# Operand addresses, matmul order and raw buffers in a hybrid decoder layer's kernel

## The chip, the cores and the metric

The kernel runs on one core of a Trainium2 chip. The metric is the device time of one execution in microseconds (us). A core has the engines TensorE (PE; its weight loads are shown apart as PEld), VectorE (DVE), ScalarE (ACT) and GpSimd (POOL), each with its own queue of instructions, and SyncE (SP), whose queue here issues the loads from memory. The engines wait for one another on semaphores.

## The reference

One decoder layer on 256 tokens of width 2048, all in float32, cut to what matters here:

```python
h = rmsnorm(x, g_mix) @ w_in                 # 2048 x 5728
z, xbc, dt, q, k, v, qi, ki, wi = _split(h, IN_SIZES)
y_ssd = gated_norm(ssd(silu(conv(xbc)), dt), z)      # 16 heads of 64
ki = rmsnorm(ki, g_kidx)                     # key of the indexer, 64 wide
y_att = dsa_attention(rmsnorm(q), rmsnorm(k), v, qi, ki, wi)   # top 64 keys
x = x + concat([y_ssd, y_att]) @ w_out       # 2048 x 2048
u = rmsnorm(x, g_mlp) @ w_up                 # 2048 x 8192
return x + square(relu(u)) @ w_down          # 8192 x 2048
```

## The kernel before

**Precision.** A float32 product is made of three products of the fast type fp32r: each operand is split into a high half (rounded) and a low half (the rest), and high·high + high·low + low·high is summed in PSUM.

**Weights.** All 400 weight tiles of the kernel come through `operands` (L110), mostly 128 x 1024 (512 KB). It has SP issue the load of `raw` (L119), ScalarE cast the high half `whi` (L122), and VectorE subtract the low half `wlo` (L123). `raw` has RB = 4 buffers, `whi` and `wlo` have WB = 5 each. So the load of a tile waits until VectorE has made the low half of the tile four before it, and the casts wait for matmuls that free `whi`. These steps have a higher priority than the rest in a scheduler that orders SP's, ScalarE's and VectorE's instructions by times of its own; TensorE's order is the order of the code.

**Products.** `product` (L126) takes the weights as the moving operand, 512 (or 304) columns, with activations loaded as 128 x 128 stationary blocks (L141 to L143). `product_t` (L168) does the reverse: a unit of 256 output columns has four tiles of eight 128 x 128 weight blocks, loaded as the stationary operand, and the activations stream past. The activations are kept as [high | low], 256 tokens each: a high weight block times both halves is one matmul of 512 columns (L181), a low block times the high half one of 256 columns (L182). A "pair" below is these two; a unit has 32 pairs.

**Stages on TensorE.** Input product in blocks: k and m0 (straight `product`; m0 is 304 wide and holds `ki`, `wi`, `dt` and part of `v`), qi (4 units) and xbc (6 units) by `product_t`, then m1, q0, q1, z0, z1 straight. Between them run the norms, the indexer, the state space part and attention, as tasks whose TensorE work enters at counted steps (`step`, the table `Y`). Then the output product (w_out), and the two layers of the MLP in quarters: `up(0)`, `up(1)`, `down(0)`, `up(2)`, `down(1)`, `up(3)`, `down(2)`, `down(3)`. `up` is 8 units of `product_t` per quarter (the very first is made ahead), `down` is straight with 512 columns.

**Addresses.** In a partition, all `whi` and `wlo` buffers start at the same byte modulo 256, as do the activations of w_out and of the down product (`yah`, `ysh`, `uh`, `ul`). `hx` (the activations of the input product) and `x2x` (those of the up product, in the same place) start 64 bytes past it.

**From m0 to qi.** After m0, ScalarE evacuates `sm0` and `sm1` (L306, scaled by `rstd`, the norm of x, which VectorE ends with L282), squares the indexer's keys (`kj`, L365, sum `kss`), VectorE turns that into a reciprocal root (`rx_ki`, L273 to L282, some dozen small operations) and writes the normed keys `kd` (L371). After the first unit of qi TensorE transposes them (`ps_ki`, L376).

Of the kernel before, what the change touches and what calls it, by code (L numbers as in the profile page):

```python
# [9 lines left out]
F32 = mybir.dt.float32  # L10
F32R = mybir.dt.float32r
# [5 lines left out]
P = 128  # L17
D = 2048
T = 256
NB = T // P  # L20
KT = D // P
# [6 lines left out]
HP = 600  # L28
WARM = 9
WB = 5  # L30
RB = 4


Z0, XBC0, DT0, Q0, K0, V0, QI0, KI0, WI0, END = (
# [31 lines left out]
def hymba_kernel(ctx: ExitStack, tc: tile.TileContext, xn, xt, w_in, w_out, w_up, w_down, vcol, vrow, out):  # L66
    nc = tc.nc
    ctx.enter_context(tc.manual_schedule(engines={nc.tensor.engine}))
    keep = ctx.enter_context(tc.tile_pool(name="keep", bufs=1))
    wts = ctx.enter_context(tc.tile_pool(name="wts", bufs=1))  # L70
# [24 lines left out]
    def step():  # L95
        for t in list(tasks):
            if isinstance(t[1], int) and t[1] > 0:
                t[1] -= 1
            elif not isinstance(t[1], str) or t[1] in done:
                advance(t)  # L100
# [6 lines left out]
        return vc[:, VC[name] + i:VC[name] + i + 1]  # L107


    def operands(src, n, load=None):  # L110

        with tc.high_priority(offset=HP):
            raw = wts.tile([P, n], F32, name="raw", tag="raw", bufs=RB)
            hi = wts.tile([P, n], F32R, name="whi", tag="whi", bufs=WB)
            lo = wts.tile([P, n], F32R, name="wlo", tag="wlo", bufs=WB)
            step = n if load is None else n // 2
            for i in range(0, n, step):
                s = slice(i, i + step)
                nc.sync.dma_start(raw[:, s], src[:, s])  # L119
                if load is not None:  # L120
                    load()
                nc.scalar.copy(hi[:, s], raw[:, s])  # L122
                nc.vector.tensor_tensor(lo[:, s], raw[:, s], hi[:, s].bitcast(F32), op=OP.subtract)  # L123
        return hi, lo
# [4 lines left out]
    def accumulators():  # L129
        return [ps.tile([P, 512], F32, name="acc", tag="acc") for _ in range(2)]  # L130

    def product(src, n, left, load=None, tail=None):
# [16 lines left out]
        for kt in range(KT):  # L149
            if kt % 2 == 0:  # L150
                hi, lo = operands(src[kt // 2], 2 * n, load)
            w = slice(kt % 2 * n, kt % 2 * n + n)
            wh, wl = hi[:, w], lo[:, w]
            if kt < last:
                part(kt, acc[0][:, :n], 0, wh, wl)
                if tail is None:
                    part(kt, acc[1][:, :n], 1, wh, wl)
                else:
                    for i, (b, c) in enumerate(halves):
                        part(kt, acc[1 + i][:, c], b, wh[:, c], wl[:, c])  # L160
            else:
                kept.append((kt, wh, wl))
            step()
# [4 lines left out]
                tail(b, c, acc[i][:, c])  # L168
        return acc

    def product_t(src, right):

        acc = accumulators()
        for i in range(4):
            hi, lo = operands(src[i], 1024)
            c = i % 2
            for k in range(8):
                kt = 8 * (i // 2) + k
                x = right(kt)
                s = slice(k * P, (k + 1) * P)  # L180
                nc.tensor.matmul(acc[c], hi[:, s], x, start=(kt == 0), stop=False)  # L181
                nc.tensor.matmul(acc[c][:, T:], lo[:, s], x[:, :T], start=False, stop=(kt == KT - 1))  # L182
                if k % 4 == 3:
                    step()
        return acc

    def total(dst, acc):

        for c in range(2):
            nc.scalar.copy(dst[:, c, :], acc[c][:, T:])  # L190
            nc.vector.tensor_tensor(dst[:, c, :], acc[c][:, :T], dst[:, c, :], op=OP.add)
# [9 lines left out]


    vc = keep.tile([P, NVC], F32, name="vc")
    hx = keep.tile([P, KT, 2 * T], F32R, name="hx")
    room = keep.tile([P, 4096], F32, name="room", tag="xr")
    
    x_done = []
# [29 lines left out]
    for name, cols in IN_BLOCKS:  # L237
        n = sum(b - a for a, b in cols)
# [8 lines left out]
    def in_pair(name, i):  # L247
        o = in_off[name][0] + i * 256 * D
        return product_t(w_in[o:o + 256 * D].rearrange("(h p c) -> h p c", h=4, p=P), lambda kt: hx[:, kt, :])
# [501 lines left out]
    def x2(kt):  # L751
        if kt >= KT - 4:
            need("res3")
        return box[0][:, kt, :]

    first = product_t(w_up[0], x2)
    while tasks:
        step()
# [11 lines left out]
    def up(q):  # L770
        uh = mlp.tile([P, KT, T], F32R, name="uh")
        ul = mlp.tile([P, KT, T], F32R, name="ul")
        for j in range(8):
            r = mlp.tile([P, 2, T], F32, name="r")
            total(r, first if q + j == 0 else product_t(w_up[8 * q + j], x2))
            nc.vector.scalar_tensor_tensor(r, r, 0.0, r, op0=OP.max, op1=OP.mult)
            s = slice(2 * j, 2 * j + 2)
            nc.scalar.copy(uh[:, s, :], r)
            nc.vector.tensor_tensor(ul[:, s, :], r, uh[:, s, :].bitcast(F32), op=OP.subtract)
        return uh, ul  # L780

    def down(q, u):
        for j in range(4):
# [9 lines left out]
            for b in range(0 if end else NB):  # L793
                add(b, slice(0, 512), acc[b])

    u = [up(0)]
    for q in range(1, 4):
        u.append(up(q))
        down(q - 1, u[q - 1])
# [53 lines left out]
```

## Time and profile before

| | |
|---|---|
| median of 3 runs | 1112.9 us (1112.73 to 1113.47) |
| the profiled execution | 1111.47 us, its span 1109.4 us |
| TensorE busy | 1100.4 us (99%) |
| VectorE, ScalarE, GpSimd busy | 692.4, 535.0, 41.4 us |
| weight loads, 512 KB, issue to landing (median) | 3.6 to 4.0 us |
| memory read | 204.29 MB, 186 GB/s over the span |

A row's duration for a matmul includes its way through the array, so neighbours overlap: a 512-column matmul is printed with 0.39 us while the next one starts 0.23 us later. Pace is therefore taken from start to start. In a timeline, equal instructions in a row may be one row with a count (x4) and the time that they take together; idle time before a row and what ended it stand in brackets.

### The profile page before, as it was taken

How to read it: one execution, taken by the hardware profiler on the slowest of the kernel's cores; microseconds unless marked ns; L12 is line 12 of the kernel's file. 1: busy time of each engine (PE TensorE's matmuls, PEld its weight loads, DVE VectorE, ACT ScalarE, POOL GpSimd, SP SyncE). 2: the span in 40 equal slices, each digit the busy share in tenths (PEclk: the TensorE clock that was granted, in tenths of full speed). 3: DMA queues.
4: the chain of work that ended last, by engine and by line, in shares of the span. 5: the costliest groups of instructions: out<-in, count | busy, mean ns of one | idle time of the engine just before them, and what ended most of it. 6: DMA issues, size and time to landing. Idle time of an engine off the chain costs nothing.

```text
span 1109.4 us, 14959 instructions
## 1 busy us (share of the span) xinstructions
PE 1100.4 (99%) x5686; PEld 937.9 (85%) x5686; DVE 692.4 (62%) x976; ACT 535.0 (48%) x749; POOL 41.4 (4%) x41
## 2 busy tenths in 40 slices
PE   9999998999999999999999999999999999999998
PEld 7988887888888888888888888888888888888887
DVE  6886989667765565656565456565555565554443
ACT  7755645556765454444443334444434444333431
POOL 0010131112000000000000000000000000000000
PEclk9999999999999999999999999999999999999999
DMA  9855435644375555556656655655666556665662
GB/s 327 270 195 175 152 106 175 194 147 134 115 256 185 184 181 184 187 189 189 183 186 198 193 190 190 191 190 190 192 192 191 188 188 191 198 195 191 209 212 73
DMA packets 63735, 207.36 MB, mean 187 GB/s; under 512 B 7216, under 2 KB 11568, under 8 KB 63664
## 3 DMA queue, kind: packets, MB, share of 16 engines
q1 hardware_dynamic: 63520, 206.36, 58.1%
q8 instruction: 45, 0.74, 0.3%
q14 instruction: 26, 0.21, 0.1%
q10 hardware_dynamic: 144, 0.05, 0.0%
HBM read 204.29 MB, written 2.10 MB: 186 GB/s over the span
## 4 chain that ended last, share of the span: by engine, by line
PE 92%; DVE 4%; DMA 1%; issue 1%; ACT 1%; SPq 0%; POOL 0%; ACTq 0%; DVEq 0%
PE acc L181 27%; PE acc L141 16%; PE acc L142 16%; PE acc L143 16%; PE acc L182 14%; DVE wlo L123 1%; DVE bc L495 1%; PE ps_y L566 1%; DVE sc L459 1%; DMA xrow<-in_xn 1%; PE ps_sr L650 0%; PE ps_l L604 0%; PE ps_o L629 0%; ACT xrow L230 0%; DMA raw<-in_w_in 0%
## 5 line engine op out<-in xcount | busy, mean ns | idle before, releaser
L123 DVE TENSOR_TENSOR wlo<-raw,whi 128x1024 fp32r<-128x1024 f32 (+3 forms) x400 | 466.9, 1170 | 380.9 <-ACT whi L122 377.7
L122 ACT CAST whi<-raw 128x1024 fp32r<-128x1024 f32 (+3 forms) x400 | 400.5, 1004 | 497.4 <-PE acc L142 248.7
L181 PE MATMUL acc<-x2x,whi 128*128 128x512 f32 x1024 | 359.9, 395 | 0.0
L182 PE MATMUL acc<-x2x,wlo 128*128 128x256 f32 x1024 | 287.8, 281 | 0.0
L181 PEld LDWEIGHTS acc<-x2x,whi 128*128 128x128 f32 x1024 | 192.5, 188 | 45.4
L142 PE MATMUL acc<-whi,ul 128*128 128x512 f32 (+1 forms) x512 | 197.6, 386 | 0.0
L141 PE MATMUL acc<-whi,uh 128*128 128x512 f32 (+1 forms) x512 | 197.5, 386 | 0.0
L143 PE MATMUL acc<-wlo,uh 128*128 128x512 f32 (+1 forms) x512 | 197.5, 386 | 0.0
L182 PEld LDWEIGHTS acc<-x2x,wlo 128*128 128x128 f32 x1024 | 192.0, 188 | 0.1
L181 PE MATMUL acc<-hx,whi 128*128 128x512 f32 x320 | 114.0, 397 | 0.0
L141 PEld LDWEIGHTS acc<-whi,uh 128*128 128x128 f32 x512 | 96.1, 188 | 19.5
L143 PEld LDWEIGHTS acc<-wlo,uh 128*128 128x128 f32 x512 | 96.1, 188 | 19.5
L142 PEld LDWEIGHTS acc<-whi,ul 128*128 128x128 f32 x512 | 96.2, 188 | 19.2
L182 PE MATMUL acc<-hx,wlo 128*128 128x256 f32 x320 | 90.0, 281 | 0.0
L143 PE MATMUL acc<-wlo,hx 128*128 128x512 f32 (+1 forms) x224 | 83.0, 370 | 3.1 <-DVE wlo L123 3.1
L141 PE MATMUL acc<-whi,hx 128*128 128x512 f32 (+1 forms) x224 | 85.4, 381 | 0.1
L142 PE MATMUL acc<-whi,hx 128*128 128x512 f32 (+1 forms) x224 | 82.6, 369 | 0.0
L181 PEld LDWEIGHTS acc<-hx,whi 128*128 128x128 f32 x320 | 60.3, 188 | 13.5
L182 PEld LDWEIGHTS acc<-hx,wlo 128*128 128x128 f32 x320 | 60.1, 188 | 0.0
L143 PEld LDWEIGHTS acc<-wlo,hx 128*128 128x128 f32 x224 | 42.0, 187 | 12.0 <-DVE wlo L123 4.7
L141 PEld LDWEIGHTS acc<-whi,hx 128*128 128x128 f32 x224 | 42.2, 188 | 7.7 <-issue 0.7
L142 PEld LDWEIGHTS acc<-whi,hx 128*128 128x128 f32 x224 | 42.1, 188 | 7.4 <-issue 0.7
(224 smaller groups left out, 828.4 us busy)
## 6 DMA issues: line engine op xcount, KB each, us to landing
raw<-in_w_up SPq DMA_DIRECT2D x128, 512.0 KB, 3.7
raw<-in_w_down SPq DMA_DIRECT2D x128, 512.0 KB, 4.0
raw<-in_w_in SPq DMA_DIRECT2D x72, 512.0 KB, 3.6
raw<-in_w_out SPq DMA_DIRECT2D x32, 512.0 KB, 3.6
raw<-in_w_in SPq DMA_DIRECT2D x16, 256.0 KB, 4.2
raw<-in_w_in SPq DMA_DIRECT2D x16, 152.0 KB, 5.3
raw<-in_w_in SPq DMA_DIRECT2D x8, 304.0 KB, 2.9
xT<-in_xt SPq DMA_DIRECT2D x16, 128.0 KB, 4.1
```

The source lines that it names most:

```text
L122: nc.scalar.copy(hi[:, s], raw[:, s])
L123: nc.vector.tensor_tensor(lo[:, s], raw[:, s], hi[:, s].bitcast(F32), op=OP.subtract)
L141: nc.tensor.matmul(out, ah[:, s], wh, start=(kt == 0), stop=False)
L142: nc.tensor.matmul(out, al[:, s], wh, start=False, stop=False)
L143: nc.tensor.matmul(out, ah[:, s], wl, start=False, stop=(kt == KT - 1))
L181: nc.tensor.matmul(acc[c], hi[:, s], x, start=(kt == 0), stop=False)
L182: nc.tensor.matmul(acc[c][:, T:], lo[:, s], x[:, :T], start=False, stop=(kt == KT - 1))
L459: nc.vector.scalar_tensor_tensor(sc[:, :nk], rl[:, i, :nk], wis[:, b, h:h + 1], neg[:, T - nk:] if first else sc[:, :nk], op0=OP.mult, op1 ...
L495: nc.vector.scalar_tensor_tensor(o[:, j, :], pad[:, j, k:k + T], vcp("conv_w", 12 * k + ct), o[:, j, :], op0=OP.mult, op1=OP.add)
L566: nc.tensor.matmul(pt[:, 64 * i:64 * i + 64], m[i // 4][:, i % 4, :], xdt[:, c, 64 * h:64 * h + 64], start=True, stop=True)
```

## The change

Three things change together.

1. **Address.** Two spare tiles in the pool, `gap0` (192 bytes) and `gap1` (64 bytes), put `hx`, and `x2x` after it, at the same byte modulo 256 as the weights. Every `whi` and `wlo` buffer gets 64 floats more; its data can start 0, 64, 128 or 192 bytes into it.
2. **The up product.** `product_t` takes a `shift` (unit j: 64·(j mod 4) bytes) and an `order`, one for each four units. H is a high block with 512 columns, l a low block with 256; X and L are the two 256-column halves of H, each with its own load of the weights. "Hl" is the order of before, "HHHHHHHHllllllll" makes the eight high matmuls of a tile and then the eight low ones. The input product keeps "Hl" and shift 0.
3. **Buffers.** `raw` has 3 buffers instead of 4, which pays for the spare floats.

```diff
--- before.py
+++ after.py
@@ -28,7 +28,11 @@
 HP = 600
 WARM = 9
 WB = 5
-RB = 4
+RB = 3
+SPARE = 64
+
+
+ORDERS = ["Hl", "HHHHHHHHllllllll", "HllH", "HHHHllll", "XLl", "XlL", "LXl", "HHll"]
 
 
 Z0, XBC0, DT0, Q0, K0, V0, QI0, KI0, WI0, END = (
@@ -107,12 +111,12 @@
         return vc[:, VC[name] + i:VC[name] + i + 1]
 
 
-    def operands(src, n, load=None):
+    def operands(src, n, load=None, shift=0):
 
         with tc.high_priority(offset=HP):
             raw = wts.tile([P, n], F32, name="raw", tag="raw", bufs=RB)
-            hi = wts.tile([P, n], F32R, name="whi", tag="whi", bufs=WB)
-            lo = wts.tile([P, n], F32R, name="wlo", tag="wlo", bufs=WB)
+            hi = wts.tile([P, n + SPARE], F32R, name="whi", tag="whi", bufs=WB)[:, shift:shift + n]
+            lo = wts.tile([P, n + SPARE], F32R, name="wlo", tag="wlo", bufs=WB)[:, shift:shift + n]
             step = n if load is None else n // 2
             for i in range(0, n, step):
                 s = slice(i, i + step)
@@ -168,19 +172,26 @@
                 tail(b, c, acc[i][:, c])
         return acc
 
-    def product_t(src, right):
+    def product_t(src, right, shift=0, order=ORDERS[0]):
 
         acc = accumulators()
         for i in range(4):
-            hi, lo = operands(src[i], 1024)
+            hi, lo = operands(src[i], 1024, None, shift)
             c = i % 2
-            for k in range(8):
-                kt = 8 * (i // 2) + k
-                x = right(kt)
-                s = slice(k * P, (k + 1) * P)
-                nc.tensor.matmul(acc[c], hi[:, s], x, start=(kt == 0), stop=False)
-                nc.tensor.matmul(acc[c][:, T:], lo[:, s], x[:, :T], start=False, stop=(kt == KT - 1))
-                if k % 4 == 3:
+            w = {"H": hi, "X": hi, "L": hi, "l": lo}
+            out = {"H": slice(0, 2 * T), "X": slice(0, T), "L": slice(T, 2 * T), "l": slice(T, 2 * T)}
+            part = {"H": slice(0, 2 * T), "X": slice(0, T), "L": slice(T, 2 * T), "l": slice(0, T)}
+            n = order.count("l")
+            for g in range(0, 8, n):
+                seen = dict.fromkeys("HXLl", 0)
+                for at, o in enumerate(order):
+                    k = g + seen[o]
+                    seen[o] += 1
+                    kt = 8 * (i // 2) + k
+                    nc.tensor.matmul(acc[c][:, out[o]], w[o][:, k * P:(k + 1) * P], right(kt)[:, part[o]],
+                                     start=(i < 2 and g == 0 and at == 0),
+                                     stop=(i >= 2 and g + n == 8 and at == len(order) - 1), skip_group_check=True)
+                for _ in range((g + n) // 4 - g // 4):
                     step()
         return acc
 
@@ -201,7 +212,9 @@
 
 
     vc = keep.tile([P, NVC], F32, name="vc")
+    keep.tile([P, 48], F32, name="gap0")
     hx = keep.tile([P, KT, 2 * T], F32R, name="hx")
+    keep.tile([P, 16], F32, name="gap1")
     room = keep.tile([P, 4096], F32, name="room", tag="xr")
     
     x_done = []
@@ -772,7 +785,7 @@
         ul = mlp.tile([P, KT, T], F32R, name="ul")
         for j in range(8):
             r = mlp.tile([P, 2, T], F32, name="r")
-            total(r, first if q + j == 0 else product_t(w_up[8 * q + j], x2))
+            total(r, first if q + j == 0 else product_t(w_up[8 * q + j], x2, 16 * (j % 4), ORDERS[2 * q + j // 4]))
             nc.vector.scalar_tensor_tensor(r, r, 0.0, r, op0=OP.max, op1=OP.mult)
             s = slice(2 * j, 2 * j + 2)
             nc.scalar.copy(uh[:, s, :], r)
```

**How it moves instructions: the entry to qi.** The scheduler orders VectorE and ScalarE anew. On VectorE, from the last step of `rstd` on (`wlo` are low halves, the first 1024-wide one is qi's first tile; `rx_ki` starts the norm of the keys), before:

```order
L282 TENSOR_TENSOR rstd<-rt_x,ry_x 128x2
L123 TENSOR_TENSOR wlo<-raw,whi 128x1024
L298 TENSOR_SCALAR dg<-ident,rstd 128x128 x2
L340 TENSOR_TENSOR s_361<-s_361,rstd 128x8
L123 TENSOR_TENSOR wlo<-raw,whi 128x1024
L340 TENSOR_TENSOR s_361<-s_361,rstd 128x8
L123 TENSOR_TENSOR wlo<-raw,whi 128x1024 x2
L372 TENSOR_SCALAR wis<-sm_106,rstd 128x16
L412 TENSOR_TENSOR dt<-sm_106,vr 128x16
L123 TENSOR_TENSOR wlo<-raw,whi 128x1024
L273 TENSOR_SCALAR rx_ki<-kss 128x2
```

and after, from the instruction behind `rstd` on:

```order
L311 TENSOR_SCALAR dg<-ident,rstd 128x128 x2
L353 TENSOR_TENSOR s_363<-s_363,rstd 128x8 x2
L127 TENSOR_TENSOR wlo<-raw,whi 128x1024 x4
L385 TENSOR_SCALAR wis<-sm_108,rstd 128x16
L385 TENSOR_SCALAR wis<-sm_109,rstd 128x16
L425 TENSOR_TENSOR dt<-sm_108,vr 128x16
L425 TENSOR_TENSOR dt<-sm_109,vr 128x16
L427 SCALAR_TENSOR_TENSOR sp_a<-dt 128x32
L127 TENSOR_TENSOR wlo<-raw,whi 128x1024
L440 TENSOR_SCALAR dt<-dt 128x32
L127 TENSOR_TENSOR wlo<-raw,whi 128x1024
L286 TENSOR_SCALAR rx_ki<-kss 128x2
```

The first low half of qi stood directly behind `rstd`; now `dg` and both scalings of `s` stand ahead of it. Up to `rx_ki` there were five low halves, now there are six.

ScalarE at the same place, from the evacuation of `sm0` on (`whi` are the high halves, here those of qi's fifth tile and later; `kj` are the squares of the keys), before:

```order
L306 ACTIVATE sm0_106<-acc_373,rstd_103 128x96
L306 ACTIVATE room_88<-acc_373,rstd_103 128x208
L122 CAST whi_778<-raw_777 128x1024
L306 ACTIVATE sm1_107<-acc_374,rstd_103 128x96
L306 ACTIVATE room_88<-acc_374,rstd_103 128x208
L365 ACTIVATE kj_586,kss_108<-sm0_106 128x64
L365 ACTIVATE kj_588,kss_108<-sm1_107 128x64
L122 CAST whi_800<-raw_799 128x1024
```

and after:

```order
L319 ACTIVATE sm0_108<-acc_375,rstd_105 128x96
L319 ACTIVATE room_90<-acc_375,rstd_105 128x208
L319 ACTIVATE sm1_109<-acc_376,rstd_105 128x96
L126 CAST whi_780<-raw_779 128x1024
L319 ACTIVATE room_90<-acc_376,rstd_105 128x208
L378 ACTIVATE kj_588,kss_110<-sm0_108 128x64
L126 CAST whi_802<-raw_801 128x1024
L378 ACTIVATE kj_590,kss_110<-sm1_109 128x64
```

The cast of `whi_802` (`whi_800` before, the sixth tile of qi) stood behind both `kj` and now stands between them. The loads on SP keep their order, but each waits for the low half of three tiles before it.

**And: the start of `up(2)` on TensorE**, the last matmuls of `down(0)` and the first of the unit (numbers are buffers), before:

```order
L141 MATMUL acc_5921<-whi_6049,uh_3994 128x512
L142 MATMUL acc_5921<-whi_6049,ul_3995 128x512
L143 MATMUL acc_5921<-wlo_6050,uh_3994 128x512
L181 MATMUL acc_6071<-x2x_3383,whi_6074 128x512
L182 MATMUL acc_6071<-x2x_3383,wlo_6075 128x256
```

and after:

```order
L145 MATMUL acc_5923<-whi_6051,uh_3996 128x512
L146 MATMUL acc_5923<-whi_6051,ul_3997 128x512
L147 MATMUL acc_5923<-wlo_6052,uh_3996 128x512
L191 MATMUL acc_6073<-x2x_3385,whi_6076 128x256 x2
L191 MATMUL acc_6073<-x2x_3385,wlo_6077 128x256
```

The matmul of 512 columns has become two of 256, in the twelve units with X and L: 384 matmuls and weight loads more.

## Rows read from the trace of the kernel before

**Rows 1.** The page: engines' busy us (share) x instructions, and clock of 40 slices in tenths.

```profile
PE 1100.4 (99%) x5686; PEld 937.9 (85%) x5686; DVE 692.4 (62%) x976; ACT 535.0 (48%) x749; POOL 41.4 (4%) x41
...
PEclk9999999999999999999999999999999999999999
```

**Rows 2.** Waits of TensorE: line, waited for, us in total, times, longest.

```profile
PE acc L143 <- DVE wlo L123: 3.1, 3, 1.8
...
PE ps_ki L376 <- DVE kd L371: 0.5, 1, 0.5
```

**Rows 3.** Timeline, TensorE, z1's last matmuls: start us, us, engine, line, op, out<-in, shape.

```profile
301.21 0.39 PE L141 MATMUL acc<-whi,hx 128*128 128x512 f32 x1
...
304.01 0.39 PE L141 MATMUL acc<-whi,hx 128*128 128x512 f32 x1
```

**Rows 4.** Timeline, TensorE, inside `down(0)`.

```profile
591.13 0.39 PE L141 MATMUL acc<-whi,uh 128*128 128x512 f32 x1
...
595.21 0.39 PE L141 MATMUL acc<-whi,uh 128*128 128x512 f32 x1
```

**Rows 5.** Timeline, TensorE, start of the output product.

```profile
305.80 0.40 PE L142 MATMUL acc<-whi,yal 128*128 128x512 f32 x1
...
307.89 0.39 PE L142 MATMUL acc<-whi,yal 128*128 128x512 f32 x1
...
312.42 0.39 PE L141 MATMUL acc<-whi,yah 128*128 128x512 f32 x1
```

**Rows 6.** Timeline, TensorE, pairs of qi.

```profile
46.77 0.40 PE L181 MATMUL acc<-hx,whi 128*128 128x512 f32 x1
...
52.43 0.39 PE L181 MATMUL acc<-hx,whi 128*128 128x512 f32 x1
```

**Rows 7.** High-half matmuls of up(0)-up(1), then up(3), by line: count, durations, first-last start.

```profile
L181 PE MATMUL acc<-x2x,whi x372: 392/397/398, 446.7 to 577.8; 128*128 128x512 f32 x186
...
L181 PE MATMUL acc<-x2x,whi x256: 392/392/398, 841.6 to 930.6; 128*128 128x512 f32 x128
```

**Rows 8.** Timeline, TensorE, 256-column matmuls at the kernel's end.

```profile
1102.91 0.28 PE L141 MATMUL acc<-whi,uh 128*128 128x256 f32 x1
...
1105.66 0.28 PE L143 MATMUL acc_t<-wlo,uh 128*128 128x256 f32 x1
```

**Rows 9.** Timeline, SP's queue, the weight loads from m0 into qi.

```profile
31.85 0.80 SPq L119 DMA_DIRECT2D raw<-in_w_in  x2
...
35.08 21.84 SPq L119 DMA_DIRECT2D raw<-in_w_in  x12
```

**Rows 10.** Timeline, ScalarE, high halves of the weights and the key norm.

```profile
38.46 1.05 ACT L122 CAST whi<-raw 128x1024 fp32r<-128x1024 f32 x1 [0.93 <-DVE ry_x L282]
40.53 1.05 ACT L122 CAST whi<-raw 128x1024 fp32r<-128x1024 f32 x1 [1.02 <-DMA raw<-in_w_in]
...
43.23 1.06 ACT L122 CAST whi<-raw 128x1024 fp32r<-128x1024 f32 x1 [0.23 <-DMA raw<-in_w_in]
...
47.21 0.25 ACT L365 ACTIVATE kj<-sm 128x64 f32<-128x64 f32 x1
```

**Rows 11.** Timeline, VectorE, low halves, key norm and `kd`.

```profile
34.19 1.63 DVE L123 TENSOR_TENSOR wlo<-raw,whi 128x304 fp32r<-128x304 f32 x4
...
37.48 0.85 DVE L123 TENSOR_TENSOR wlo<-raw,whi 128x304 fp32r<-128x304 f32 x2
...
39.93 1.23 DVE L123 TENSOR_TENSOR wlo<-raw,whi 128x1024 fp32r<-128x1024 f32 x1
...
47.69 0.16 DVE L273 TENSOR_SCALAR rx_ki<-kss 128x2 f32<-128x2 f32 x1
...
53.42 0.41 DVE L371 TENSOR_SCALAR kd<-sm,krs 128x64 f32<-128x64 f32 x2
```

**Rows 12.** Timeline, TensorE, the first matmuls of the kernel.

```profile
1.26 4.16 PE L200 MATMUL ps_w<-ones 128*128 128x128 f32 x18 [1.26 <-POOL ones L195]
...
5.54 0.50 PE L142 MATMUL acc<-whi,hx 128*128 128x512 f32 x1
```

## The prediction

> **What bounds the kernel now.** I read the page first: TensorE is busy 99% of the span, and the granted clock stands at its top digit in every slice [rows 1]. So an edit counts only if it changes how long TensorE's own matmuls take, or if it makes TensorE wait. Next come the waits of TensorE: three of 3.1 us in all on VectorE's low halves of the weights, and one of 0.5 us at the transposes of `kd` [rows 2]. Everything else TensorE has in time. The rest is read as pace: the distance from the start of one matmul to the start of the next, since the printed duration overlaps the neighbour.
>
> Three paces matter. With `hx` as the moving operand, 64 bytes past the weights' place in 256, twelve matmuls of 512 columns take 304.01 − 301.21 = 2.80 us, 233.3 ns each [rows 3]. In the down product, where activations and weights have the same place, eighteen take 4.08 us, 226.7 ns [rows 4]. The difference, 6.6 ns, is what the new addresses are worth at most. It isn't had at once: after the transposes ahead of the output product, where the places are also equal, the first nine take 2.09 us (232 ns), the next twenty 4.53 us (226.5) [rows 5].
>
> **The offsets in the input products.** `hx` moves to the weights' place. The straight blocks after the m1 block have 384 matmuls of 512 columns (q0, q1, z0, z1). All at the lower pace is 384 × 6.6 ns = 2.5 us. But work of other kinds (transposes, attention) interrupts them some 24 times in TensorE's order, and each time about nine run at 232: 216 × 1.3 ns + 168 × 6.6 ns = 1.4 us. I take −1.4, with 0 and −2.5 as ends. The 96 of the k block gain 0.6 us, which is worth nothing: what follows waits for VectorE (below). The 320 pairs of qi and xbc take 353.8 ns at first (16 in 5.66 us) [rows 6]. Locked, a pair would be 226.7 + 120 = 346.7. I take half of that gap, 3.3 ns, for the 288 pairs behind the wait below: −0.95, ends 0 and −2.0.
>
> **The pairs of the up product.** Of its 32 units of 32 pairs, 16 (quarters 0 and 1) now run at 131.1/371 = 353.4 ns a pair, 16 (quarters 2 and 3) at 89.0/255 = 349.0 [rows 7], all with one offset and one order. Since one offset has two paces, offset alone doesn't set it. Afterwards 20 units stay unsplit, in four orders and four offsets. The ends for the 16 early ones are the locked pair, 512 × 6.7 ns = −3.4 us, and a pace as much worse, +3.4; I take half the gain, −1.7, because a quarter of the units get the equal place and most get longer runs of one shape. The four late ones sit near 349.0 whatever happens: 0, ends ±0.3.
>
> **The split units.** Twelve units (three half quarters) split the 512-column matmul in two of 256 that load the same weights twice: 384 more matmuls and 384 more weight loads. A pair then costs three of 256. At the end of the kernel 23 of these follow one another in 2.75 us, 119.6 ns each [rows 8]: 358.7 against 349.0, 9.7 ns × 384 = +3.7 us. The ends: 349.0 − 233.3 = 115.7 for a 256 next to a 512 gives 347.1 and −0.7; 353.4 − 226.7 = 126.7 gives 380 and +11.9. I take +3.7, from the row with the same shape back to back.
>
> **Three raw buffers instead of four.** Now each load waits on SP for the low half of the tile four before; then for that of three before. In the steady stretches a tile feeds TensorE for 2.8 us (eight pairs at 350, or twelve at 233), while landing, high half and low half take 3.4 + 1.05 + 1.23 = 5.7 us [rows 9 to 11]; three buffers give one tile in 1.9 us, so it stays hidden there. It doesn't at the entry to qi. I follow it tile by tile, numbering tiles from the kernel's start; 32 is the first of qi.
>
> Before, the last two loads of m0 (30, 31) are issued at 31.85 [rows 9]; the low halves 24 to 27 run from 34.19 to 35.82, and 31 is done at 38.33 [rows 11]. After, these loads wait for 26 and 27, so they go out at about 35.4 and 35.8 and land some 3.4 us later (issue at 35.08 to the cast at 38.46 [rows 9, 10] bounds it). High and low halves of 304-wide pairs bring tile 31 to about 39.6, 1.3 us late. VectorE's order makes it worse. The small operations of `rstd`, which ended just ahead of 39.93 [rows 11], now end near 40.7, and in the new order `dg` and the two scalings stand before tile 32, so its low half comes at 41.4 to 42.6 instead of 39.93 to 41.16. TensorE wants it at 41.8: first wait, 0.8 us.
>
> Load 35 waits for that, goes out at 42.7 instead of 38.36, and lands at about 46.1. Its cast was at 43.23 [rows 10]; now it ends at 47.15, and behind it in ScalarE's order stand `sm1`, the cast of 36, the first `kj`, the cast of 37, and only then the second `kj`, which releases the norm. `kj` before ran at 47.21 [rows 10]. Casts 36 and 37 end at 48.6 and 50.75, so `kj` ends near 51.0. VectorE has the low half of 37 ahead of `rx_ki`: 52.0 instead of 47.69. From there to the last `kd` it needed 53.83 − 47.69 = 6.1 us, with two low halves (37, 38) and a string of small operations [rows 11]; the new order has two low halves inside as well (38, 39) and about as many small ones. So `kd` is done near 58.2 to 58.5, not 53.83. TensorE, whose order is the code's, waits at the transposes of `kd`, and all matmuls of qi behind them wait with it; before, it could go on at once at 53.83. That is **+4.7 us** including the 0.8 above. With landings of 3.0 us it is +3.5, with 4.7 (load 33, issued at 35.85, cast at 40.53 [rows 10]) up to +6.
>
> Behind that everything is later alike. In the m1 block, where TensorE waits 3.1 us today [rows 2], loads that come one tile later add between 0 and 3.1; I take +0.5, as the wait there is on VectorE's own queue.
>
> **Sum.** +4.7 − 0.95 − 1.4 − 1.7 + 3.7 + 0.5 = +4.85 us. The profiled execution took 1111.47 us (span 1109.4) and would take 1116.3; the median of the runs is 1112.9, 1.4 above it, and gives **1117.7 us**, +0.4%. Anything within 0.2% (2.2 us) counts as no change: about what can be told here.
>
> **Rivals.**
> *The addresses don't matter.* Then the lower pace of the down product comes from something else (its shape, no 256 in between), and the three gains fall away: 1112.9 + 4.7 + 3.7 + 0.5 = 1121.8. Against it: the output product settles at the same 226.5 with other data and other neighbours [rows 5]. For it: the up pairs have two paces at one offset [rows 7]. Chance 0.12. The Trainium skill would side with this one: its page "SBUF — State Buffer", section "Who interferes with whom", gives TensorE two independent read ports, one for the moving operand and one for weight loads, and says that it never waits on anyone. The trace has 233.3 against 226.7 at one shape, so for the terms I go by the rows.
>
> *The clock falls.* At the start TensorE works slowly: 18 passes of 128 columns last from 1.26 to 5.42, and the 512-column matmul at 5.54 still prints 0.50 us [rows 12] where later ones print 0.39 [rows 3]; that is the lower of its two levels (1.2 and 2.4 GHz). If the idle time at the `kd` transposes sends it there again, for as long as at the start (1.26 to 5.54, 4.3 us), half of that is lost: 2.1 us, 1119.8. The page's clock row doesn't show the slow start, and no wait before is longer than 1.8 us [rows 2], so the trace can't decide. Chance 0.13. The skill's page "TensorE: Matmul & The Clock Gate", section "Why this matters for your kernels", warns that an idle gap between bursts of matmuls can bring the lower level back; no run here shows that yet.
>
> *The entry stays hidden.* If load 35 reaches ScalarE as early as before, `kj` stays near 47.5 and `kd` near 54: the +4.7 shrinks to at most 0.5, and gains and split cancel: 1113.0 to 1113.5, no change. For it: TensorE waits only 0.5 there now. Against it: the three steps that delay it (loads, VectorE's order, ScalarE's order) stand one behind the other. Chance 0.20.
>
> *Everything locks: faster.* If with equal or new offsets and longer runs each matmul takes the lower pace, the ends add: −2.0 − 2.5 − 3.4 − 0.3 − 0.7, against +4.7 + 0.5: 1112.9 − 3.7 = 1109.2. It decides once the pace terms together pass −7.4. Against it: nine matmuls after each interruption don't lock [rows 5], and the pairs interrupt themselves. Chance 0.10.
>
> *Bad offsets.* If 128 or 192 bytes, or two loads of one weight, cost as the upper end of the split says: +8.2 more, 1126. Chance 0.05.
>
> **How the numbers follow.** The forecast has 0.40; its own range, by landing times and the pair's ends, is 1114.5 to 1120.5. The range to 1122 takes in the clock and most of the dead addresses; down to 1111 the hidden entry; about 0.17 is left out. Slower: 0.35 of the forecast, 0.13, 0.12, 0.05 = 0.65. Faster: 0.10 and 0.02 of the hidden entry. The same: 0.23.
>
> **What will show it.** In the profile after: the wait of TensorE at the transposes of `kd` (right: 3 to 6 us; wrong: below 1), with the second `kj` near 51 us; `hx` matmuls of the z blocks at 226.7 once settled (wrong: 233); split pairs of quarter 2 at 358 ns and not 349 or 380; pairs of quarters 0 and 1 near 350, by unit; no new wait over 1 us in the up stretches. If the time falls below 1112 while the wait is there, the pair terms were undersized.

## The result and the profile after

The changed kernel takes 1121.43 us (median of 4 runs, 1120.63 to 1122.1) against 1112.82 before: a ratio of 1.0079, 95% interval 1.0067 to 1.0092. It is slower by 8.6 us, with the sign forecast, but the forecast was 3.7 us too low. The time lies near the upper end of the range given, and above the 1114.5 to 1120.5 that the forecast's own terms allowed; the range reached it only because it was widened for two rivals, so that it holds is in part luck. The size went wrong most at the entry, by more than the 3.7 us; other terms made up for part of it. In two of the experiments below one execution took thousands of microseconds (6282 and 3497 us), and their medians are given without it.

The page of the changed kernel, which answers to [rows 1] (span in us; busy us, share, instructions by engine):

```profile
span 1118.7 us, 15733 instructions
...
PE 1101.6 (98%) x6070; PEld 957.2 (86%) x6070; DVE 691.4 (62%) x976; ACT 534.8 (48%) x749; POOL 42.2 (4%) x41
```

The span is 9.3 us longer than before, and TensorE is busy only 1.2 us longer, though it makes 384 matmuls more. So nearly all of it is waiting. The waits of TensorE (line, what it waited for, us, times, longest), against [rows 2]:

```profile
PE ps_ki L389 <- DVE kd L384: 5.5, 1, 5.5
PE acc L147 <- DVE wlo L127: 2.1, 2, 1.8
PE acc L191 <- ACT whi L126: 1.5, 1, 1.5
PE acc L145 <- ACT whi L126: 1.3, 2, 0.9
```

The wait at the transposes of `kd`, 0.5 us before, is 5.5 us; waits for the weights of m0 and of qi's first unit are new (the last two lines). How the rest moved is read by stretch, from the start of each product in both traces (us, the profiled executions, 9.3 in all):

| stretch | forecast | measured |
|---|---|---|
| k, m0 and entry to qi, up to the end of its second unit | +4.7 | +10.4 |
| the rest of qi and xbc | −0.95 | +0.2 |
| m1 | +0.5 | +0.4 |
| q0, q1, z0, z1 | −1.4 | −1.8 |
| output product | 0 | +0.3 |
| up(0), up(1), no unit split | −1.7 | −2.2 |
| twelve split units of up(2), up(3) | +3.7 | +2.2 |
| four unsplit units of up(3) | 0 | −0.2 |

**The entry.** The chain went the way that the prediction laid out, and later at each step. ScalarE and VectorE, timelines (start us, us, line, operation, idle time before it in brackets), against [rows 10, 11]:

```profile
43.78 1.04 ACT L126 CAST whi<-raw 128x1024 fp32r<-128x1024 f32 x1 [3.54 <-DMA raw<-in_w_in]
...
51.13 1.05 ACT L126 CAST whi<-raw 128x1024 fp32r<-128x1024 f32 x1 [3.66 <-DMA raw<-in_w_in]
...
55.31 0.27 ACT L378 ACTIVATE kj<-sm 128x64 f32<-128x64 f32 x1
```

```profile
36.24 1.63 DVE L127 TENSOR_TENSOR wlo<-raw,whi 128x304 fp32r<-128x304 f32 x4
...
44.86 2.50 DVE L127 TENSOR_TENSOR wlo<-raw,whi 128x1024 fp32r<-128x1024 f32 x2 [2.15 <-ACT whi L126]
...
56.60 0.16 DVE L286 TENSOR_SCALAR rx_ki<-kss 128x2 f32<-128x2 f32 x1
...
62.43 0.57 DVE L384 TENSOR_SCALAR kd<-sm,krs 128x64 f32<-128x64 f32 x3
```

ScalarE twice stands idle for a load, for 3.5 and for 3.7 us: for qi's first tile (load 32) and for the fourth (load 35). SP issued them here:

```profile
38.07 1.23 SPq L123 DMA_DIRECT2D raw<-in_w_in  x2
...
46.11 0.33 SPq L123 DMA_DIRECT2D raw<-in_w_in  x1
```

From issue to cast that is 43.78 − 38.07 = 5.7 us and 51.13 − 46.11 = 5.0 us, where the prediction had taken 3.4. From `rx_ki` on the chain took 63.0 − 56.6 = 6.4 us (6.1 forecast).

**The clock.** While TensorE was idle and just behind it, the windows read (from:to, length, busy us of PE, PEld, DVE, ACT, POOL; then granted clock, share of the DMA engines, GB/s):

```profile
60.00:62.00 2.00, 0.00 (x0) 0.00 (x0) 2.00 (x17) 1.01 (x3) 0.00 (x0) 1.00 0.74 203
62.00:64.00 2.00, 1.27 (x5) 1.03 (x6) 2.00 (x11) 0.66 (x2) 0.00 (x0) 0.64 0.53 147
64.00:66.00 2.00, 2.00 (x8) 1.71 (x8) 2.00 (x6) 0.00 (x0) 0.54 (x1) 0.51 0.60 229
66.00:68.00 2.00, 2.00 (x13) 1.74 (x13) 1.07 (x3) 0.59 (x1) 2.00 (x2) 1.00 0.77 248
```

A granted clock of 0.51 is the lower level, 1.2 of 2.4 GHz. TensorE's own timeline shows what it costs:

```profile
62.73 0.80 PE L389 MATMUL ps_ki<-ident,kd 128*128 128x128 f32 x2 [5.46 <-DVE kd L384]
63.19 0.77 PE L191 MATMUL acc<-hx,whi 128*128 128x512 f32 x1
...
65.25 0.63 PE L191 MATMUL acc<-hx,whi 128*128 128x512 f32 x1
...
65.89 0.43 PE L191 MATMUL acc<-hx,whi 128*128 128x512 f32 x1
```

A pair takes 0.64 us instead of 0.35. The four pairs from 63.19 to 65.89 take 2.70 us instead of 4 × 0.35 = 1.40, so 1.3 us are lost. The rival with the clock came true on top of the forecast, at a price of 1.3 and not 2.1 us. The page "TensorE: Matmul & The Clock Gate" of the Trainium skill says in its section "Why this matters for your kernels" that an idle gap between bursts of matmuls brings the lower level; this trace agrees at the wait of 5.46 us.

But such a long gap is not needed. In the same trace the clock fell a second time, in m1, behind a wait of 1.77 us:

```profile
184.39 0.41 PE L147 MATMUL acc<-wlo,hx 128*128 128x304 f32 x1 [1.77 <-DVE wlo L127]
...
186.00:188.00 2.00, 1.66 (x7) 1.29 (x7) 1.95 (x7) 0.00 (x0) 0.38 (x1) 0.50 0.28 108
```

In the trace of before the same wait left it at the upper level:

```profile
173.79 0.41 PE L143 MATMUL acc<-wlo,hx 128*128 128x304 f32 x1 [1.77 <-DVE wlo L123]
...
174.00:176.00 2.00, 1.74 (x12) 1.49 (x11) 1.90 (x8) 0.00 (x0) 0.00 (x0) 1.00 0.53 152
```

So the length of the wait alone doesn't decide. That section of the Trainium skill warns of longer gaps than this one; the measurement decides. In m1 no loss can be told from it: with four buffers (experiment 2) the clock falls there too, and m1 takes 19.7 us as before, where it doesn't fall; in the changed kernel m1 takes 20.1.

**The paces.** z1 now runs locked, against [rows 3]: six matmuls in 1.36 us, 226.7 ns.

```profile
311.91 0.39 PE L145 MATMUL acc<-whi,hx 128*128 128x512 f32 x1
...
313.27 0.39 PE L145 MATMUL acc<-whi,hx 128*128 128x512 f32 x1
```

In the up product each unit has a steady pace of its own. In ns a pair, worked out from the starts (the distance is that of the activations past the weights, modulo 256 bytes; it is 256 bytes less the shift, so shifts of 64, 128, 192 are the distances 192, 128, 64):

| units 0-3 / 4-7 of | order | distance 0 | 192 | 128 | 64 |
|---|---|---|---|---|---|
| up(0), first half | Hl | 353.3 (the first of all, where no other work interrupts it) | 353.3 | 350.6 | 348.9 |
| up(0), second half | HHHHHHHHllllllll | 349.1 | 347.1 | 351.2 | 344.8 |
| up(1), first half | HllH | 348.7 | 346.9 | 348.6 | 345.2 |
| up(1), second half | HHHHllll | 350.3 | 346.8 | 351.4 | 347.0 |
| up(2), first half | XLl | 359.7 | 353.4 | 356.1 | 353.4 |
| up(2), second half | XlL | 360.0 | 340.7 | 355.8 | 353.3 |
| up(3), first half | LXl | 359.7 | 353.4 | 356.1 | 353.4 |
| up(3), second half | HHll | 348.8 | 347.2 | 348.1 | 345.9 |

One cell is out of line: three matmuls of 256 in 340.7 ns, less than any unit that isn't split, at a distance where the same three take 353.4 in two other units. The low matmuls of units 4 and 5 of up(2), 22 pairs in 7.92 us and 23 pairs in 7.82 us (360.0 and 340.0):

```profile
719.96 0.28 PE L191 MATMUL acc<-x2x,wlo 128*128 128x256 f32 x1
...
727.88 0.29 PE L191 MATMUL acc<-x2x,wlo 128*128 128x256 f32 x1
...
731.39 0.28 PE L191 MATMUL acc<-x2x,wlo 128*128 128x256 f32 x1
...
739.21 0.28 PE L191 MATMUL acc<-x2x,wlo 128*128 128x256 f32 x1
```

### The profile page after: what moved, and what is told of

Read it like the earlier page. It is cut to its first block, busy times and chain, and to the rows that moved or that the text cites. A ratio compares the mean times of both kernels' runs of the same rounds, so it can differ in the third digit from the quotient of the medians.

```text
span 1118.7 us, 15733 instructions
## 1 busy us (share of the span) xinstructions
PE 1101.6 (98%) x6070; PEld 957.2 (86%) x6070; DVE 691.4 (62%) x976; ACT 534.8 (48%) x749; POOL 42.2 (4%) x41
## 4 chain that ended last, share of the span: by engine, by line
PE 91%; DMA 3%; DVE 3%; ACT 1%; issue 1%; SPq 0%; POOL 0%; ACTq 0%; DVEq 0%
PE acc L191 40%; PE acc L145 16%; PE acc L147 15%; PE acc L146 15%; DMA raw<-in_w_in 2%; DVE wlo L127 1%; PE ps_y L579 1%; ACT whi L126 1%; DMA xrow<-in_xn 1%; DVE sc L472 1%; DVE bc L508 0%; PE ps_sr L663 0%; PE ps_l L617 0%; PE ps_o L642 0%; DMA xT<-in_xt 0%
## 5 line engine op out<-in xcount | busy, mean ns | idle before, releaser
L191 PE MATMUL acc<-x2x,whi 128*128 128x256 f32 (+1 forms) x1408 | 328.5, 332 | 0.0
L191 PEld LDWEIGHTS acc<-x2x,whi 128*128 128x128 f32 x1408 | 225.8, 189 | 12.9
L191 PE MATMUL acc<-x2x,wlo 128*128 128x256 f32 x1024 | 232.0, 280 | 0.0
L191 PEld LDWEIGHTS acc<-x2x,wlo 128*128 128x128 f32 x1024 | 181.3, 188 | 15.2
```

The source lines that it names most:

```text
L191: nc.tensor.matmul(acc[c][:, out[o]], w[o][:, k * P:(k + 1) * P], right(kt)[:, part[o]], start=(i < 2 and g == 0 and at == 0), stop=(i >= ...
```

## The experiments

Two questions: is the missing fourth buffer the cause of the entry, and what sets the pace of a pair. The experiments count from 1 in the order below.

### One buffer less, alone

```diff
-RB = 4
+RB = 3
```

> The kernel before with 3 raw buffers and nothing else. Theory A (the third raw buffer alone makes the delay from m0 into qi, by later loads and the order of VectorE and ScalarE that follows from it): the start of qi's second unit is 9 to 11 us later than before, with a wait of TensorE at the transposes of kd of 4 to 6 us and a low granted clock behind it; nothing else moves by over 0.5 us; 1112.8 + 10.7 = about 1123. Theory B (the delay comes from the shifted weights or the new address of the activations, which slow loads or casts): the wait at kd stays under 1 us and the time under 1114.

Measured: 1122.48 us against 1112.71, ratio 1.0085 (1.0070 to 1.0100). Its waits of TensorE:

```profile
PE ps_ki L376 <- DVE kd L371: 5.5, 1, 5.5
PE acc L143 <- DVE wlo L123: 2.1, 2, 1.8
```

Theory A holds: the second unit of qi starts 9.7 us later than before, the third 10.8, m1 adds 0.6, and from q0 on nothing moves by over 0.1 us. The granted clock behind the wait is again at the lower level:

```profile
63.00:65.00 2.00, 1.82 (x6) 1.49 (x7) 2.00 (x11) 0.00 (x0) 0.00 (x0) 0.50 0.53 170
```

The buffer alone costs 9.8 us, more than the whole change. It also makes the new order: VectorE's instructions of this kernel stand as those of the changed one (but for a few), and those of the next kernel as those of before.

### All the rest, with four buffers

```diff
-RB = 3
+RB = 4
-    jp = keep.tile([P, P], I32, name="jp")
+    jp = mid.tile([P, P], I32, name="jp", **u2)
```

(against the changed kernel; `jp` goes into a shared buffer for want of 256 bytes)

> The changed kernel with 4 raw buffers; 256 bytes are won by putting the mask's helper jp into a buffer of the pool of norms, nothing else. Theory A: entry to qi as before, so 1121.4 - 10.7 - 0.4 (m1) = about 1110.3, which is faster than before by 0.2%; the up units keep the paces of the changed kernel (344.8 to 360 ns a pair). Theory B: the delay stays, over 1119.

Measured: 1111.39 us, ratio to before 0.9981 (0.9972 to 0.9991). That is 10.0 us less than the changed kernel. The up units repeat their paces to 0.1 ns. Theory A, but for one point: the entry is not as before here. It is 2.9 us later than in the profile of before at qi's third unit, with these waits, and the time is 1.1 us above the one expected:

```profile
PE ps_ki L389 <- DVE kd L384: 2.0, 2, 1.1
...
PE acc L145 <- ACT whi L126: 0.5, 1, 0.5
```

The next kernel, with the order of before throughout, is 2.3 us late there as well; other kernels with four buffers (below) 0.0 to 2.3. So with four buffers the entry differs by up to 3 us between profiled executions, and that of before was an early one (1111.47 against a median of 1112.9). What the buffer costs is therefore taken from the medians: 9.8 us in one comparison, 10.0 in the other.

### The addresses alone

```diff
+    keep.tile([P, 48], F32, name="gap0")
     hx = keep.tile([P, KT, 2 * T], F32R, name="hx")
+    keep.tile([P, 16], F32, name="gap1")
```

> The kernel before with the two spare tiles alone, so that hx and x2x stand at the weights' address modulo 256; 4 raw buffers, one order, no shifts. Theory A (the equal address helps matmuls with 512 moving weight columns and not the pairs): q0 to z1 give 1.8 us as in the changed kernel, qi and xbc nothing, and the up pairs in the plain order take 349 to 354 as before: 1111 to 1112.8. Theory C (in the plain order equal addresses slow the pairs: the first unit of up took 357.8 ns there): up costs 512 x 4.4 ns + 512 x 8.8 ns = 6.8 us, minus 1.8: about 1117.8. Theory D (pairs lock at 346.7): 1112.8 - 1.8 - 3.4 - 1.1 = 1106.5.

Measured: 1113.35 us, ratio 1.0007 (0.9997 to 1.0017), no change that can be told. By stretch: q0 to z1 −1.8 us, qi and xbc behind the entry +0.2, up(0) and up(1) 0.0, up(2) and up(3) +2.3, since every up unit behind the first now takes 352.8 to 353.5. Its pairs in up(2), 23 in 8.13 us, where before they took 349:

```profile
669.74 0.28 PE L182 MATMUL acc<-x2x,wlo 128*128 128x256 f32 x1
...
677.87 0.28 PE L182 MATMUL acc<-x2x,wlo 128*128 128x256 f32 x1
```

So equal places help the straight products, where all matmuls have 512 columns, and not the pairs of the up product. Theory A holds but for up(2) and up(3); C and D fall. (C rested on 357.8 ns for the first up unit of all, which was no pace: transposes of another task stand between its pairs, and where nothing interrupts them they take 353.3.)

### The wait at `kd` taken away

```diff
-        yield 7
+        yield 15
```

(in `index_keys` of the changed kernel: TensorE makes eight steps more, one unit of qi, before the transposes)

> The changed kernel with the transposes of kd eight steps later in TensorE's order, behind the second unit of qi instead of the first; 3 raw buffers. Theory A (of the delay, 5.0 us are idle time at kd and about 1.5 us the lower clock behind it): both go, no stretch of qi has a low granted clock: 1121.4 - 6.5 = about 1115. Theory E (the loads are late anyway, the wait moves to the weights of the second unit): TensorE waits for high or low halves there and the time stays over 1118.

Measured: 1113.37 us, 8.1 less than the changed kernel; between the two profiled executions it is 6.2 (6.5 expected). Theory A holds: the wait at `kd` is gone, and no new one is longer than 0.3 us:

```profile
PE acc L147 <- DVE wlo L127: 1.8, 1, 1.8
...
PE acc L145 <- ACT whi L126: 1.2, 2, 0.9
PE acc L191 <- ACT whi L126: 1.1, 1, 1.1
```

and the granted clock stays at the upper level where it fell before:

```profile
62.00:64.00 2.00, 2.00 (x13) 1.77 (x12) 2.00 (x7) 1.09 (x2) 0.00 (x0) 1.00 0.54 203
64.00:66.00 2.00, 2.00 (x15) 1.82 (x14) 2.00 (x7) 1.05 (x1) 1.41 (x1) 1.00 0.81 242
```

Most of the buffer's price is therefore one dependence that TensorE's fixed order can't step around, with the lower clock behind it. What is left, some 3.9 us at the start of qi's second unit, is the late weights of m0 and of qi's first unit.

### XlL at 64 bytes in all units

```diff
-product_t(w_up[8 * q + j], x2, 16 * (j % 4), ORDERS[2 * q + j // 4])
+product_t(w_up[8 * q + j], x2, 16, "XlL")
```

(the first unit, made ahead, too; a shift of 64 bytes is the distance 192; from here on with four buffers)

> The changed kernel with 4 raw buffers, and all 32 up units in the order XlL with their weights shifted 64 bytes (as unit 5 of up(2), which took 340.7 ns a pair there). Theory F (order and offset set the pace): every unit takes 340.7, up costs 1024 x 340.7 ns = 348.9 us against 359.5 before: 1112.7 - 10.6 - 1.8 (straight blocks) = about 1100. Theory G (that unit was a chance state that hangs on the unit ahead of it): the units take 353 to 360 as the other split ones: 1112.7 - 1.8 + 2 to 5 = 1113 to 1116.

Measured: 1106.86 us, ratio 0.9939 (0.9920 to 0.9958). Both theories are half right: from the second unit on, up(0) and up(1) take 340.0 ns a pair in every unit, up(2) and up(3) 353.3 in every unit. Twenty pairs of up(1) in 6.80 us, then twenty of up(2) in 7.07 us:

```profile
486.92 0.28 PE L191 MATMUL acc<-x2x,wlo 128*128 128x256 f32 x1
...
493.72 0.28 PE L191 MATMUL acc<-x2x,wlo 128*128 128x256 f32 x1
...
660.75 0.28 PE L191 MATMUL acc<-x2x,wlo 128*128 128x256 f32 x1
...
667.82 0.28 PE L191 MATMUL acc<-x2x,wlo 128*128 128x256 f32 x1
```

The instructions and the distance are the same in both; what differs is the place in the kernel and what ran ahead, the first unit behind the output product or `down(0)`.

### The grouped order at 192 bytes in all units

```diff
+product_t(w_up[8 * q + j], x2, 48, "HHHHHHHHllllllll")
```

> The changed kernel with 4 raw buffers, and all 32 up units in the order of eight high matmuls and then eight low ones, weights shifted 192 bytes, which is the distance of before (as unit 7 of up(0), 344.8 ns a pair in the changed kernel). Theory F: 344.8 in all units: 359.5 - 353.1 = 6.4 us less, and 1.8 us in the straight blocks: about 1104.5. Theory G: 349 to 353 in most units: 1110 to 1112.

Measured: 1105.99 us, ratio 0.9937 (0.9917 to 0.9956). A shift of 192 bytes is the distance 64 of before. All units but the first take 344.6. The first one lost 1.2 us: eight high matmuls in a row want the last activations sooner than they are there (TensorE waits 0.9 us for `x2x`). Theory F holds for this pair of order and distance.

### A grid of orders and distances

Eight orders for four units each, shifts of 0, 64, 128, 192 bytes in turn.

> The changed kernel with 4 raw buffers; eight orders (XlL, lXL, LlX, XXllLL, XXXXllllLLLL, XLlLXl, lH, llllllllHHHHHHHH) for four units each with shifts of 0, 64, 128, 192 bytes. Theory F: XlL repeats 360.0, 340.7, 355.8, 353.3 by shift though it now stands in up(0), and the other orders differ by shift by up to 20 ns a pair. Theory G: XlL at 64 bytes takes 353 or more here.

Measured (one execution): 1114.0 us, neither theory. XlL took 353.4 at 64 bytes in the first half of up(0); lXL, behind it, 340.6. All six split orders have the same pace at one distance to 0.4 ns (359.7 or 360.0 at 0, 356.1 or 355.8 at 128, 353.3 or 353.4 at 64; the very first unit aside), but for the distance 192, where it is 353.4 in units 1 of up(0) and up(2) and 340.6 in units 5 of both and in units 1 and 5 of up(1). So among split orders the order counts for nothing; the distance counts, and what ran before.

This trace also bears on the clock: behind a wait of 1.13 us at the transposes of `kd` it fell to the lower level. The kernel with units of another kind in between (below) has the same wait there, 1.13 us, and keeps the upper level.

```profile
54.78 0.33 PE L389 MATMUL ps_ki<-ident,kd 128*128 128x128 f32 x1 [1.13 <-DVE kd L384]
...
56.00:58.00 2.00, 2.00 (x8) 1.71 (x7) 2.00 (x4) 0.00 (x0) 0.00 (x0) 0.50 0.56 207
```

### The order alone

The kernel before with `HHHHHHHHllllllll` in the 31 units made inside `up`, nothing else.

> The kernel before with one edit: the 31 up units made inside up take eight high matmuls and then eight low ones of a tile; 4 raw buffers, no gaps, no shifts, activations 64 bytes past the weights. Theory F (the order sets the pace at this distance): 344.6 ns a pair in all 31 units, 15 x 32 x 8.7 ns + 16 x 32 x 4.3 ns = 6.4 us less: 1106.4. Theory H (the gain needs the other parts, or is a state that the entry decides): 348.9 to 353.3 in one half: over 1109.

Measured: 1106.09 us, ratio 0.9939 (0.9920 to 0.9958): 344.6 in all of them but the three that follow other work (346.3 to 346.5). From one unit's start to the next, 32 pairs in 11.03 us:

```profile
695.94 2.00 PE L191 MATMUL acc<-x2x,whi 128*128 128x512 f32 x8
...
706.97 0.39 PE L191 MATMUL acc<-x2x,whi 128*128 128x512 f32 x1
```

Theory F. This single edit of an order is worth 6.2 us and needs no memory.

### Units of another kind in between

up(0), up(1): plain order at the old distance, unit 4 of up(0) at 0. up(2): XlL with 64 bytes, unit 4 at 0. up(3): a grouped unit with 192 bytes, then XlL with 64.

> The changed kernel with 4 raw buffers and other units. up(0), up(1): the plain order Hl with weights shifted 192 bytes (the distance of before) but unit 4 of up(0) with no shift. up(2): XlL with 64 bytes, unit 4 with no shift. up(3): unit 0 grouped with 192 bytes, then XlL with 64 bytes. Theory K (each distance has two steady paces, and what stands ahead picks one, which then stays): up(0) 353.3 in units 1 to 3 and 348.9 from unit 5 on; up(2) 353.3 in units 0 to 3 and 340.0 to 340.6 from unit 5 on; up(3) 340 or 353.3 throughout. Theory L (the place in the kernel decides, not the unit ahead): 353.3 in all of up(0) and up(1), 353.3 in all of up(2) but unit 4.

Measured (one execution): 1110.79 us. A unit at distance 0 changes nothing: the units of up(0) and up(1) behind it stay at 353.2 to 353.5, up(2) at 353.3 behind it. A grouped unit does: the XlL units behind it in up(3) take 340.6 and then 340.0, here 17 pairs in 5.78 us:

```profile
856.93 0.28 PE L195 MATMUL acc<-x2x,wlo 128*128 128x256 f32 x1
...
862.71 0.28 PE L195 MATMUL acc<-x2x,wlo 128*128 128x256 f32 x1
```

Two steady paces at one distance, one of which what stands ahead picks and which then stays: that part of K holds. That any unit of another distance tips it falls; and so does L, which was right for up(0) to up(2): up(3), behind `down(1)`, has the quick pace here, where it had 353.3 with XlL in all units.

### What is best of it, together

up(0), up(1) XlL with 64 bytes; up(2), up(3) grouped with 192; the transposes of `kd` eight steps later.

> The changed kernel with 4 raw buffers, the transposes of kd eight steps later, up(0) and up(1) in the order XlL with 64 bytes, up(2) and up(3) grouped with 192 bytes. From the runs before: up(0), up(1) at 340.0 and up(2), up(3) at 344.6 ns a pair give 16 x 32 x 13.3 + 16 x 32 x 4.3 ns = 9.0 us, the straight blocks 1.8, the wait at kd up to 1: 1112.8 - 11 = about 1102. If the state at the entry is another one, up(0) and up(1) take 353.3: 1108.

Measured: 1100.9 us, ratio to before 0.9886 (0.9863 to 0.9909).

Then, in up(2) and up(3), only the first unit grouped and XlL with 64 bytes behind it:

> As the combined kernel, but in up(2) and up(3) only the first unit grouped with 192 bytes, and the seven behind it in the order XlL with 64 bytes. Theory K2 (a grouped unit ahead picks the quicker of the two paces, as in up(3) of the run before): 340.0 in all of these, 14 x 32 x 4.6 ns = 2.1 us less than the combined kernel: about 1098.8. Rival (behind down(0) they fall to 353.3 in up(2) as they did with XlL alone): 7 x 32 x (8.7 - 4.6) ns = 0.9 us more: 1101.8.

Measured: 1098.51 us, ratio 0.9868 (0.9848 to 0.9887), against 1098.8 expected: 340.6 in the unit right behind the grouped one and 340.0 in all others, here 23 pairs in 7.82 us.

```profile
681.90 0.28 PE L191 MATMUL acc<-x2x,wlo 128*128 128x256 f32 x1
...
689.72 0.28 PE L191 MATMUL acc<-x2x,wlo 128*128 128x256 f32 x1
```

Without the grouped unit ahead the same units of up(2) and up(3), at the same place, took 353.3 (all XlL, above). So the unit ahead picks the pace, and not the place. This kernel is 14.6 us faster than the one before, and 22.9 than the changed one.

## Why the prediction was right or wrong

**The entry, +4.7: right place and mechanism, half the size (+10.4).** The cut from four buffers to three alone makes it (experiment 1), through the loads, the orders of VectorE and ScalarE and the norm of the keys, and TensorE waits at `kd`. Three steps were too small.

First, the landing. The prediction took 3.4 us from issue to cast, the quickest row it had [rows 9, 10], and kept 4.7 for the upper end; in the trace after it is 5.7 for qi's first tile and 5.0 for load 35, which both lie in the chain. The first left VectorE idle for 2.15 us, the second is 1.6 us more than forecast.

Second, the loads at the end of m0. The kernel has 400 loads but 384 tiles: the 16 tiles of k and m0 come in two halves each. The prediction had numbered halves as tiles, and had loads 30 and 31 wait for 26 and 27; they belong to one buffer, which with three buffers waits for the tile of 24 and 25, and went out behind it at 37.13 instead of 35.4. The slip itself is worth little, since by the times of [rows 11] the right tile was done near 35.1. What counted is that its low half was 2.05 us later than in [rows 11] (36.24 against 34.19). It starts at 34.07 to 36.43 in the profiles with four buffers and at 36.24 to 37.35 in those with three, so most of the lateness occurs without the change; whether the missing buffer adds to it is not shown. It fits with a difference of the two profiled executions at the entry, 10.4 us, that is more than the buffer's 9.8 to 10.0 by the medians, m1 included.

Third, the clock. It was a rival with a chance of 0.13, and it came on top: 1.3 us. The wait that the forecast itself asked for can bring it; the two should not have been priced as alternatives.

The sum of it, against the chain on record: the low half of qi's first tile starts at 44.86 instead of 41.4, the cast of load 35 at 51.13 instead of 46.1, and `kd` is done at 63.0 instead of 58.2 to 58.5. These 4.6 us and the 1.3 of the clock make up nearly the 5.7 that were missing.

**The equal addresses.** For the straight blocks, −1.4 forecast, −1.8 measured, shown three times over (changed kernel, experiments 2 and 3). So the interruptions must have cost less than nine slow matmuls each. For the pairs of qi and xbc half a lock was taken, −0.95; it was +0.2, nothing. The step that failed was to price equal places as half a lock throughout. The locked pair exists: in the first unit of qi of the changed kernel twenty pairs take 6.93 us, 346.5 ns each.

```profile
48.79 0.39 PE L191 MATMUL acc<-hx,whi 128*128 128x512 f32 x1
...
55.72 0.39 PE L191 MATMUL acc<-hx,whi 128*128 128x512 f32 x1
```

But that unit takes 353.0 in the kernel of experiment 2, at the same distance, and later units of qi and xbc take up to 354 in both. Equal addresses alone (experiment 3) give 353.3 in up, the slower of the two old paces.

**The unsplit units, −1.7: −2.2.** The sum was near, the reason half wrong. The prediction expected the gain from the equal place and from longer runs of one shape; the table of paces shows that it is the runs of one shape: at the old distance of 64 the orders that group take 344.8 to 347.0, at distance 0 348.7 to 350.3. A part is neither: unit 3 of up(0), with the old order at the old distance, takes 348.9 where it took 353.2 before, the other of the two old paces. Grouping alone, all eight by eight, gives 6.2 us (experiment 8).

**The split units, +3.7: +2.2.** The price of three 256-column matmuls, 119.6 [rows 8], was right for distance 0 (119.9) only; at the others it is 117.8 to 118.7, and 113.6 in one unit. The upper end of 380 ns was empty.

**m1, +0.5:** +0.4 in the changed kernel, +0.6 with the buffer alone.

**The rivals.** "The addresses don't matter" gave the time nearest to the measured one (1121.8), for the wrong reason: the straight blocks refute it, the pairs of qi and xbc fit it. The rule behind it, in the Trainium skill's page "SBUF — State Buffer", section "Who interferes with whom", has TensorE wait on nobody; no trace here says what makes the pace differ by address, only that it does (226.7 against 233.3 ns in z1 with nothing else changed, experiment 3). "The entry stays hidden" needed load 35 to be on time; it was 7.9 us late. "Everything locks" was too timid in a way: 340.0 lies under the 346.7 that it called locked, but only in units that this kernel mostly doesn't have.

**What stays open.** What the state is that picks one of two paces (353.3 or 348.9 for plain pairs at the distance 64 in the kernel before, 353.3 or 340.0 for split ones at the distance 192), and why a grouped unit ahead picks the quick one where `down` and a unit at distance 0 don't. The runs show that it repeats in another kernel with the same units (before and experiment 1, the changed kernel and experiment 2) and is carried from unit to unit; they don't show where it lies. Open too is why one wait of 1.13 or 1.77 us is followed by the lower clock and the next of the same length is not.

## What to carry to other kernels

A buffer less in a load pipeline is priced at the one place where it is entered from other work, not by the steady state; use at least the slowest landing that the trace shows near that place, and follow the scheduler's new orders up to the first instruction on the busy engine that cannot be moved. Where TensorE's order is fixed, moving a waiting step behind work that is ready (here eight steps) can give back most of what the buffer costs, here 8.1 of some 10 us, as the clock stays up there as well. For long rows of alternating matmul shapes, group equal shapes and measure the pace from start to start by unit: it is steady to a fraction of a nanosecond and depends on order, on address and on what ran ahead, so one profiled run with a different setting for each unit is a grid of experiments, if the units' history is kept in mind.

## What the runs showed of the hardware that was not expected

- The pace of fp32r matmuls depends on the distance of the moving operand from the stationary one modulo 256 bytes: 226.7 ns at 0 against 233.3 at 64 for 512 columns with a new weight block each; for 256 columns three in a row take 353.4 ns at 64, 355.8 at 128 and 360.0 at 0.
- At one distance and one order there can be two steady paces, 340.0 and 353.3 ns for three matmuls at the distance 192, and which one holds is decided by the work ahead and then kept over hundreds of matmuls.
- Three matmuls of 256 columns with three weight loads (340.0 ns) can be quicker than one of 512 and one of 256 with two (344.6 at best).
- TensorE's granted clock fell to its lower level behind an idle gap of 5.46 us, but also behind one of 1.77 us (0.50 from 186 to 188 us in the changed kernel) and one of 1.13 us (0.50 from 56 to 58 us in the grid), while the same gaps left it at 1.00 in other runs (1.77 us before, 1.13 us in the run with units of another kind).
